# x by ScalarE's queue, first weights in 256 KB pieces, state-space parameters later: a change to the start of a decoder layer's kernel

## The chip, the cores and the metric

The kernel runs on one core of a Trainium2 chip. The core has five engines that run on their own and wait for one another through semaphores: TensorE (PE: matrix products; PEld in the profile is its loading of the stationary operand), VectorE (DVE), ScalarE (ACT), GpSimd (POOL) and SyncE (SP, which here only issues DMAs). DMAs are issued by SP, ACT or POOL from their instruction streams and are carried by 16 DMA engines.

The metric is device time in microseconds (us). Before the change the median of three runs is 1703.63 us.

## The reference

One layer of a decoder on 256 tokens of 2048 numbers. x is multiplied with one wide matrix, three token mixers (S5, GLA, HGRN2) work on the columns, gates merge them, and an MLP follows. Cut to what matters here:

```
h = x @ W_in                        # (256, 2048) @ (2048, 14352), float32
y_a = s5_branch(u_a, lam_re, lam_im, log_dt, b_re, b_im, c_re, c_im, ...)
y_b = gla_branch(q_b, k_b, v_b, ...)        y_c = hgrn2_branch(q_c, f_c, i_c, ...)
merged = sum over branches of sigmoid(gate) * (y @ W_up)
x = layer_norm(alpha * x + merged @ W_out)
x = layer_norm(alpha * x + relu(x @ W1)**2 @ W2)
```

The change touches only the order in which x, the first columns of W_in and the parameters of S5 arrive.

## The kernel before, in words

All products are float32 products made of rounded parts: an operand is split into a high part (ScalarE copies it to a rounded type, `act`, L129) and a low part (VectorE subtracts, `tt`, L107), and three products (high with high, high with low, low with high) give the result. The weights stream through the core once. They come in loads of 1 MB (`emit_dma`, L169 for the first four and L172 for all others), into four raw buffers (NRAW = 4). Each load has two halves of 512 KB, and each half is split (`emit_split`, `emit_lower`) some steps before its products.

The program is one list of steps, written out in order. A step is the products of one half of a load with one of the two token tiles. The first chunk of the list is 512 columns of W_in (the values of GLA): four loads, eight halves, 16 steps of six products each (L1321 to L1323). The chunks that follow it are of the other kind, with 128 columns at a time on the partitions (L1326, L1327).

x has to be turned around before it can be used. `load_x` (L246) loads it in eight pieces of 256 columns (256 KB, 1 KB for each token), and `x_piece` takes one piece through four transposes on TensorE (`transposes`, L134), a copy on ScalarE (L129) and a subtraction on VectorE (L107). The first piece is done ahead of step 0, the seven others in every second step from step 1 to step 13. While the first operands arrive, TensorE multiplies zeros (WARM = 4 products, L228; the profile counts each as two).

At the start SP issues everything that the stream needs: the identity matrix for the transposes (L138), and then by turns one piece of x and half a load of weights, sixteen DMAs in all. GpSimd issues the norm weights of HGRN (`hnw`, L1258), the parameters of S5 (`s5_params`, L279 to L294, thirteen DMAs) and two masks (`load_masks`, L584 and L585).

The work of the token mixers is done by background tasks. They are Python generators; `run_tasks` lets them emit instructions, by priority, as long as an estimate of what VectorE and ScalarE have been given stays below 1240 ns a step. `yield n` makes a task wait for 2 n steps. In the kernel before, `s5_params` issues its DMAs with its first instruction and yields 3; its next part begins with a transpose of the small vectors (L298) on TensorE. `s5_prepare` and `s5_main` wait until `s5_params` is through; the result of S5 is used when its sigmoid unit (`split_z`, `in_s_w_glu_dram`) begins.

Each engine carries out its instructions in the order in which they are emitted, DMA issues among them.

Of the kernel before, what the change touches and what calls it, by code (L numbers as in the profile page):

```python
# [24 lines left out]
WARM = 4           # products of zeros at the start  # L25

# columns of w_in
# [3 lines left out]
# 2*pi in parts of few bits, so that their products with a whole number are exact  # L31
# [7 lines left out]
class Chunk:  # L39
    """A product of weights with activations that are split into rounded parts.  # L40
    rows: 512 columns of the result for each of the two token tiles, tokens on partitions;
    cols: two blocks of 128 columns of the result, these on partitions;
    low: the one block of 16 columns (with 112 that are not used), on partitions."""

    def __init__(self, units, act, evac, kind="rows"):
        self.units = units        # DRAM views [128, k-tiles, columns] of 1 MB
        self.act = act            # k-tile -> its parts
        self.evac = evac          # evac(t, psum)
        self.kind = kind
        self.kpu = units[0].shape[1]  # L50
        self.groups = [[u] for u in range(len(units))]   # units that take tile 0 before tile 1
        self.ps = {}
# [3 lines left out]
def trunk_kernel(ctx: ExitStack, tc, io, out):  # L56
    nc = tc.nc
    V, S, G, T = nc.vector, nc.scalar, nc.gpsimd, nc.tensor

    # ------------------------------------------------------------------ pools  # L60
# [7 lines left out]
    WPG = 8            # pages kept for the weights  # L68
# [27 lines left out]
    # --------------------------------------------- instructions with their cost  # L96
# [34 lines left out]
    def transposes(ps, srcs):  # L131
        """ps [128, 512]: up to four [128, 128] blocks side by side"""
        for i, s in enumerate(srcs):
            T.transpose(ps[:, i * 128:(i + 1) * 128], s, ident)  # L134

    # -------------------------------------------------------------- constants
    ident = cst.tile([128, 128], F32, name="ident")
    nc.sync.dma_start(ident, io["c_eye"])  # L138
    xin = io["x"][0].rearrange("(t p) d -> p t d", p=128)

    w_in = io["w_in"][0]
# [4 lines left out]
    # ---------------------------------------------------------- weight stream  # L146
# [3 lines left out]
    loads = []          # (chunk, ku): 4x128 rows of weights in order of first use  # L150
    order = []          # (chunk, ku, j): halves of them
    steps = []          # (chunk, ku, j, t)
# [4 lines left out]
    def emit_dma():  # L157
        k = dma_n[0]
        if k >= len(loads):
            return  # L160
        c, ku = loads[k]
        r = wp.tile([128, 4, 512], F32, tag="raw", bufs=NRAW, name=f"raw{k}")
        n = c.units[ku].shape[2]
        r4 = r.rearrange("p a b -> p (a b)").rearrange("p (k n) -> p k n", n=n)
        raws[id(c), ku] = r
        dma_n[0] += 1
        if k < NRAW:
            for j in range(2):
                nc.sync.dma_start(r4[:, 2 * j:2 * j + 2], c.units[ku][:, 2 * j:2 * j + 2])  # L169
                yield  # L170
        else:
            nc.sync.dma_start(r4, c.units[ku])  # L172

    late = {}            # the lower parts, a step after the upper ones
# [20 lines left out]
    def emit_lower(n):  # L195
        """those of the halves before n"""
        for k in [k for k in late if k < n]:
            late.pop(k)()

    # ------------------------------------------------------- background tasks  # L200
    tasks = []           # [priority, ready step, generator]
# [13 lines left out]
    def run_tasks(vb, sb):  # L215
        """urgent ones (priority < 0) always; others while the budgets last"""
# [6 lines left out]
    # keep the array busy while the first operands arrive: its clock rises with use  # L223
# [6 lines left out]
    # ------------------------------------------------------ x, its transposes  # L230
    xq = {}          # pairs of k-tiles: [128, 2, (hi, lo), 256 tokens]

    def parts(pages):
        """k-tile -> (hi, lo, both side by side) of pages that hold pairs of k-tiles"""
# [7 lines left out]
    def load_x(ku):  # L242
        xn[ku] = page((128, 2, 512))
        for i in range(2):
            c0 = ku * 512 + i * 256
            nc.sync.dma_start(xn[ku][:, :, i * 256:i * 256 + 256], xin[:, :, c0:c0 + 256])  # L246
            yield

    def split_from_psum(hi, lo, ps, t):
        """psum [128, 4*128] -> columns of token tile t of the pages hi, lo"""  # L250
# [5 lines left out]
    def x_piece(q):  # L256
        """k-tiles 2q, 2q + 1"""
# [10 lines left out]
    # ------------------------------------------------------------ S5 constants  # L268
    S5 = {}

    def s5_params():
        tmp0, tmp1 = page((128, 8, 128)), page((128, 8, 128))
        w = [tmp0[0:32, i, :] for i in range(8)]
# [22 lines left out]
        # per-partition vectors  # L296
# [5 lines left out]
        # lower bound of the forget gates: softmax over the one layer, its running sum less the first  # L302
# [11 lines left out]
        # discretisation, [32 pairs of groups, 128 states]  # L314
# [13 lines left out]
        # the whole number in two parts of few bits  # L328
# [10 lines left out]
        # turns once more into [-1/2, 1/2]  # L339
# [37 lines left out]
        # sine and cosine of theta*t for t = 0..15 and t = 0, 16..240, [128, 2, 32 pairs, 16]  # L377
# [21 lines left out]
        # input matrices [128 = (group of the pair, state), re/im, 32 pairs, 16]  # L399
# [14 lines left out]
        # block-diagonal expansions of four pairs at a time  # L414
# [6 lines left out]
    def s5_prepare():  # L421
        """for each two pairs the stacked operands of B u, which carry float32 products in one
        pass of rounded parts: u as [hi; lo; hi], B^T as [hi; hi; lo], 32 rows each"""
# [44 lines left out]
    uT = {}          # batch-of-four -> page [128 channels, 4, 256]  # L468
    zT = {}
    zq = {}  # L470
    yT = {}          # branch -> {ku: (hi, lo)}

    def s5_tables(hb):
        """sine and cosine of theta*t, [128, 2 pairs, 256], by the sum of angles"""
# [16 lines left out]
    def s5_main():  # L491
# [4 lines left out]
        for hb in range(16):  # L496
# [38 lines left out]
            # s_re = cos zr - sin zi ; -s_im = -cos zi - sin zr  # L535
# [41 lines left out]
    # ------------------------------------------------- gated linear attention  # L577
    masks = {}

    def load_masks():  # L580
        m = cst.tile([128, 5, 128], U8, name="lvl")
# [3 lines left out]
        G.dma_start(dg, io["c_diag"])  # L585
        masks["m"], masks["d"] = m, dg
# [7 lines left out]
    def attention(Q, K, A, need, vsrc, dv, sink):  # L594
        """Q, K, A [128 k, 4 heads, 256 t]; vsrc(t, h) -> [128, dv]; scores by halves of
        blocks of doubling size, each against the decay to the middle of its block. Blocks of
        up to 32 sit side by side on the columns of the array."""
# [92 lines left out]
    def squares(ss, blocks):  # L690
        """sums of squares of blocks [128, n] into the columns of ss"""
# [5 lines left out]
    def rms(ss, n):  # L697
        """1/sqrt(mean of squares + eps)"""
# [5 lines left out]
    def transpose_out(nat, hi, lo, t):  # L704
        """nat [128 tokens, 512] -> columns of tile t in pages hi, lo"""
# [4 lines left out]
    R = {}     # results kept between tasks  # L710

    # GLA -----------------------------------------------------------------
    def ev_copy(key, c, func=AF.Copy, scale=None, dve=False):
        """natural chunk into a page [128, 2, 512]"""
# [6 lines left out]
    def joined(ps, o, scale=None):  # L721
        """o = the two halves of a bank added: products with the high and the low parts"""
# [8 lines left out]
    def ev_page(key, i, func=None, scale=None):  # L731
        """two blocks of columns into blocks 2i, 2i+1 of a page [128, 4, 256 tokens]"""
# [25 lines left out]
    def ev_low(t, ps):  # L758
        """low-rank decay logits, transposed [16, 256]"""
# [6 lines left out]
    def gla_decay(glT):  # L766
        """the decays of GLA, [128, 4 heads, 256]"""
# [51 lines left out]
    # HGRN ----------------------------------------------------------------  # L819
    def ev_f(g, i):  # L820
        """forget gates f of two heads, keys 1 - f"""
# [42 lines left out]
    def branch_out(br):  # L864
        """natural results of a branch to pages with the columns on partitions"""
# [16 lines left out]
    # merge ---------------------------------------------------------------  # L882
# [30 lines left out]
    # ------------------------------------------------------------ layer norms  # L913
# [28 lines left out]
    def normalise(which, t, mv, rs, dve, pool):  # L942
        """rows of tile t; the chunks of dve there, those of pool on ScalarE and GpSimd"""
# [53 lines left out]
    # -------------------------------------------------------------------- MLP  # L997
    hid = {}

    def ev_mlp1_rows(hc):  # L1000
        """512 hidden columns, tokens on partitions"""
# [15 lines left out]
    def ev_mlp1(hc, i):  # L1017
        """blocks 2i, 2i+1 of 512 hidden columns, these on partitions"""
# [39 lines left out]
    # ------------------------------------------------------------ the program  # L1058
    xact = parts(xq)

    def named(pages):
        """k-tile -> parts, of pairs of pages (hi, lo) of four k-tiles"""
# [72 lines left out]
    # sigmoid unit of branch A, columns on partitions  # L1135
# [85 lines left out]
    # pages are released when the last chunk that reads them has been issued  # L1221
# [28 lines left out]
    # start: x and the first weights  # L1250
    for _ in range(NRAW):
        for _ in zip(load_x(dma_n[0]), emit_dma()):
            pass
# [4 lines left out]
    G.dma_start(hnw, io["hgrn_norm_w"].to_broadcast([128, 128]))  # L1258
# [24 lines left out]
    for s, (c, ku, j, t) in enumerate(steps):  # L1283
# [28 lines left out]
        nj = kpu // 2                       # k-tiles in these pages  # L1312
# [36 lines left out]
def _constants():  # L1349
    """depend on shapes alone: identity, which group of a pair a channel row is in, the time  # L1350
    index, and for each block size the pairs (key in first half, query in second half)"""
# [36 lines left out]
```

## Time and profile before

| | before |
|---|---|
| device time, three runs | 1703.1, 1704.76, 1703.63 us; median 1703.63 us |
| span of the profiled execution | 1702.4 us (first to last instruction; the profile gives no other time for it) |
| TensorE busy | 1671.8 us, 98% of the span |
| VectorE, ScalarE, GpSimd busy | 1202.0, 817.3, 190.1 us |
| mean granted TensorE clock | 0.993 of full speed |
| DMA | 318.6 MB, 187 GB/s on average |

A profile is one execution, with times from its first instruction on. A row of a timeline is the start, the duration, the engine (SPq, ACTq, POOLq and POOL's DMA rows are DMA issues), the line of the kernel, the operation, the output and the input by their names in the program, and how many such instructions the row merges. In brackets stands how long the engine had been idle before, and what ended that. The time of a DMA issue is the time the issuing engine spends on it; "to landing" is from the issue to the semaphore that says that all data has arrived. The busy time of TensorE is modelled, since its products are pipelined.

### The profile page before, as it was taken

The page shows a single profiled execution, that of the slowest core. Times are in us where ns is not written, and L with a number is a line of the kernel's source. Part 1 is how long each engine was busy: PE and PEld are TensorE (multiplying, and loading weights), DVE is VectorE, ACT ScalarE, POOL GpSimd, SP SyncE. Part 2 cuts the span into 40 slices and gives each one's busy share as a digit, 9 for nine tenths or more (in the row PEclk, how much of TensorE's full clock was granted, in tenths as well). Part 3 has the DMA queues.
Part 4 walks back from the last instruction along what each step waited for, and adds up shares of the span by engine and source line. Part 5 has one row for each costly group of instructions (what it writes and reads, how often), then busy time and mean ns, then how long its engine had stood idle before and what let it go on. Part 6 is the DMA issues. An engine that isn't in the chain of part 4 may idle for free.

```text
span 1702.4 us, 23554 instructions
## 1 busy us (share of the span) xinstructions
PE 1671.8 (98%) x9390; PEld 1386.8 (81%) x9390; DVE 1202.0 (71%) x1568; ACT 817.3 (48%) x1141; POOL 190.1 (11%) x133
## 2 busy tenths in 40 slices
PE   8999999999999999999999999999999999999996
PEld 6887788887877878878888878888888888888885
DVE  5978889698999999975675756555555555555556
ACT  4463554464535444434644436454455545454540
POOL 2132211021322322100000200000000000000002
PEclk9999999999999999999999999999999999999998
DMA  9555455554556555656585546656655555656651
GB/s 287 188 168 186 154 177 183 159 178 158 179 165 206 187 182 192 204 190 210 168 283 210 179 135 202 194 187 198 198 179 187 188 188 198 198 178 190 226 198 49
DMA packets 218301, 318.61 MB, mean 187 GB/s; under 512 B 8644, under 2 KB 117536, under 8 KB 218192
## 3 DMA queue, kind: packets, MB, share of 16 engines
q1 hardware_dynamic: 213920, 309.43, 55.2%
q10 hardware_dynamic: 3568, 6.46, 1.2%
q0 software_dynamic: 704, 1.24, 0.5%
q8 instruction: 73, 1.20, 0.3%
q14 instruction: 36, 0.29, 0.1%
HBM read 308.70 MB, written 2.10 MB: 183 GB/s over the span
## 4 chain that ended last, share of the span: by engine, by line
PE 90%; DVE 6%; DMA 2%; issue 1%; ACT 1%; SPq 0%; DVEq 0%; ACTq 0%
PE acc L1326 20%; PE acc L1321 19%; PE acc L1323 18%; PE acc L1322 18%; PE acc L1327 10%; DVE pg L107 3%; DMA raw<-in_w_in_dram 1%; DVE hf L107 1%; PE m L552 1%; PE m L134 1%; DVE pg L118 1%; PE m L623 1%; DVE hf L532 1%; ACT pg L129 0%; PE pb L508 0%
## 5 line engine op out<-in xcount | busy, mean ns | idle before, releaser
L107 DVE TENSOR_TENSOR pg<-raw,pg 128x1024 fp32r<-128x1024 f32 (+1 forms) x571 | 708.6, 1258 | 78.5 <-ACT pg L129 37.5
L129 ACT ACTIVATE pg<-raw 128x1024 fp32r<-128x1024 f32 (+1 forms) x571 | 582.5, 1051 | 318.4 <-PE acc L1323 147.2
L1321 PE MATMUL acc<-pg,pg 128*128 128x512 f32 x1504 | 596.8, 397 | 7.4 <-ACT pg L129 4.7
L1323 PE MATMUL acc<-pg,pg 128*128 128x512 f32 x1504 | 589.0, 392 | 2.4 <-DVE pg L107 2.3
L1322 PE MATMUL acc<-pg,pg 128*128 128x512 f32 x1504 | 589.1, 392 | 2.3 <-DVE pg L107 2.2
L1326 PE MATMUL acc<-pg,pg 128*128 128x512 f32 x1552 | 549.3, 399 | 0.0
L1327 PE MATMUL acc<-pg,pg 128*128 128x256 f32 x1552 | 435.6, 281 | 0.0
L1326 PEld LDWEIGHTS acc<-pg,pg 128*128 128x128 f32 x1552 | 291.7, 188 | 71.7 <-issue 0.7
L1321 PEld LDWEIGHTS acc<-pg,pg 128*128 128x128 f32 x1504 | 283.3, 188 | 71.7 <-ACT pg L129 5.9
L1323 PEld LDWEIGHTS acc<-pg,pg 128*128 128x128 f32 x1504 | 283.5, 189 | 63.6 <-DVE pg L107 3.4
L1322 PEld LDWEIGHTS acc<-pg,pg 128*128 128x128 f32 x1504 | 283.6, 189 | 60.9 <-DVE pg L107 5.4
L1327 PEld LDWEIGHTS acc<-pg,pg 128*128 128x128 f32 x1552 | 293.6, 189 | 0.6
L129 ACT ACTIVATE hf<-acc 128x256 f32<-128x256 f32 (+2 forms) x103 | 39.8, 386 | 206.5 <-PE acc L1327 195.7
L107 DVE TENSOR_TENSOR hf<-acc,hf 128x256 f32<-128x256 f32 (+1 forms) x69 | 29.1, 421 | 139.6 <-ACT hf L129 139.6
L951 POOL TENSOR_TENSOR pg<-pg,hf 128x512 f32<-128x512 f32 x7 | 11.4, 1623 | 973.1 <-ACT pg L129 973.1
L107 DVE TENSOR_TENSOR hf<-hf,hf 128x512 f32<-128x512 f32 (+1 forms) x144 | 116.5, 827 | 3.5 <-ACT hf L129 1.6
L107 DVE TENSOR_TENSOR pg<-pg,acc 128x512 f32<-128x512 f32 x56 | 38.3, 684 | 90.2 <-PE acc L1323 90.2
L129 ACT ACTIVATE hf<-hf 128x256 f32<-128x256 f32 (+1 forms) x152 | 68.3, 456 | 23.2 <-DMA hf<-pg 20.4
L129 ACT ACTIVATE pg<-acc 128x512 f32<-128x512 f32 x40 | 23.8, 595 | 115.8 <-PE acc L1323 115.8
L107 DVE TENSOR_TENSOR pg<-pg,pg 128x512 f32<-128x512 f32 (+3 forms) x75 | 51.4, 715 | 26.0 <-PE m L623 13.6
L129 ACT ACTIVATE pg<-m 128x512 fp32r<-128x512 f32 (+3 forms) x51 | 24.6, 502 | 73.5 <-PE m L134 54.4
L107 DVE TENSOR_TENSOR hf<-pb,hf 128x256 f32<-128x256 f32 x128 | 46.4, 414 | 18.7 <-issue 11.6
(129 smaller groups left out, 739.8 us busy)
## 6 DMA issues: line engine op xcount, KB each, us to landing
raw<-in_w_in_dram SPq DMA_DIRECT2D x109, 1024.0 KB, 5.1
raw<-in_w_mlp_in_dram SPq DMA_DIRECT2D x64, 1024.0 KB, 5.8
raw<-in_w_mlp_out_dram SPq DMA_DIRECT2D x64, 1024.0 KB, 5.1
raw<-in_w_up_dram SPq DMA_DIRECT2D x24, 1024.0 KB, 5.1
raw<-in_w_out_dram SPq DMA_DIRECT2D x16, 1024.0 KB, 6.4
raw<-in_w_in_dram SPq DMA_DIRECT2D x8, 512.0 KB, 11.2
raw<-in_s_w_glu_dram SPq DMA_DIRECT2D x4, 1024.0 KB, 6.0
hf<-pg SPq DMA_DIRECT2D x96, 32.0 KB, 3.3
```

What stands on the lines that cost most here:

```text
L107: V.tensor_tensor(o, a, b, op=op)
L118: V.scalar_tensor_tensor(o, a, s, b, op0=op0, op1=op1)
L129: S.activation(o, a, f, **kw)
L134: T.transpose(ps[:, i * 128:(i + 1) * 128], s, ident)
L532: V.tensor_tensor_scan(z[:, i, :], S5["mag"][:, j:j + 1].to_broadcast([128, 256]), z[:, i, :], 0.0, ALU.mult, ALU.add)
L552: T.matmul(yps[r, 0:256], lhsT=W[:, 2 + ri, r], rhs=m[:, i, :], start=ri == 0, stop=ri == 1)
L623: T.matmul(ps[32 * c:32 * c + 32, i * 16:(i + 1) * 16], lhsT=Kf[:, r], rhs=q4[:, :, 1, :], start=True, stop=True)
L1321: T.matmul(ps, lhsT=a[0][:, sl], rhs=wh[:, i, :], start=f, stop=False)
L1322: T.matmul(ps, lhsT=a[0][:, sl], rhs=wl[:, i, :], start=False, stop=False)
L1323: T.matmul(ps, lhsT=a[1][:, sl], rhs=wh[:, i, :], start=False, stop=l)
L1326: T.matmul(ps, lhsT=wh[:, i, n], rhs=a[2], start=f, stop=False)
L1327: T.matmul(ps[:, 0:256], lhsT=wl[:, i, n], rhs=a[0], start=False, stop=l)
```

## The change

The identity matrix and all of x are issued by ScalarE instead of SP. For each of the first four loads, the two pieces of x come first, then the weights: the first load in four pieces of 256 KB, the three others in halves as before. There is one more product of zeros. `s5_params` and `load_masks` begin with a wait of ten steps; the first DMA of `s5_params` writes a buffer of which VectorE sets one column to zero first, so that GpSimd's DMAs start behind that instruction of VectorE. The DMA of `hnw` goes behind those of the masks. Comment lines are left out here, and nothing else differs.

```diff
-WARM = 4
+WARM = 5
...
     ident = cst.tile([128, 128], F32, name="ident")
-    nc.sync.dma_start(ident, io["c_eye"])
+    S.dma_start(ident, io["c_eye"])
...
         if k < NRAW:
-            for j in range(2):
-                nc.sync.dma_start(r4[:, 2 * j:2 * j + 2], c.units[ku][:, 2 * j:2 * j + 2])
+            n = 1 if k == 0 else 2
+            for j in range(0, 4, n):
+                nc.sync.dma_start(r4[:, j:j + n], c.units[ku][:, j:j + n])
                 yield
...
             c0 = ku * 512 + i * 256
-            nc.sync.dma_start(xn[ku][:, :, i * 256:i * 256 + 256], xin[:, :, c0:c0 + 256])
-            yield
+            S.dma_start(xn[ku][:, :, i * 256:i * 256 + 256], xin[:, :, c0:c0 + 256])
...
     def s5_params():
+        yield 5
         tmp0, tmp1 = page((128, 8, 128)), page((128, 8, 128))
+
+        V.memset(tmp1[0:32, 0, 0:1], 0.0)
...
     def load_masks():
+        yield 5
...
         G.dma_start(dg, io["c_diag"])
+        G.dma_start(hnw, io["hgrn_norm_w"].to_broadcast([128, 128]))
...
-    for _ in range(NRAW):
-        for _ in zip(load_x(dma_n[0]), emit_dma()):
-            pass
+    for k in range(NRAW):
+        load_x(k)
+        list(emit_dma())
...
-    G.dma_start(hnw, io["hgrn_norm_w"].to_broadcast([128, 128]))
     x_piece(0)
     emit_split()
```

## Rows read from the trace of the kernel before

**Rows 1.** The page: busy time of each engine, share of the span, instructions
```profile
PE 1671.8 (98%) x9390; PEld 1386.8 (81%) x9390; DVE 1202.0 (71%) x1568; ACT 817.3 (48%) x1141; POOL 190.1 (11%) x133
```
**Rows 2.** Busy time by stretch: length, engines, PEclk, DMA share, GB/s
```profile
6.00:8.00 2.00, 0.00 (x0) 0.00 (x0) 0.69 (x1) 0.36 (x1) 0.58 (x1) 1.00 0.99 355
...
10.00:12.00 2.00, 2.00 (x5) 1.47 (x6) 0.49 (x2) 1.06 (x1) 2.00 (x2) 0.50 1.08 362
```
**Rows 3.** Timeline of the start: zeros, x's first piece, first weights, first products
```profile
1.19 3.78 PE L228 MATMUL m<-wz 128*128 128x256 f32 x8 [1.19 <-DVE epsl L688]
...
4.76 0.96 PE L134 MATMUL m<-ident,pg 128*128 128x128 f32 x4
...
5.76 0.60 ACT L129 ACTIVATE pg<-m 128x512 fp32r<-128x512 f32 x1 [3.74 <-PE m L134]
...
8.35 1.15 ACT L129 ACTIVATE pg<-raw 128x512 fp32r<-128x512 f32 x2 [1.99 <-DMA raw<-in_w_in_dram]
...
9.03 0.79 PE L1321 MATMUL acc<-pg,pg 128*128 128x512 f32 x1 [3.31 <-ACT pg L129]
...
12.54 0.48 PE L1321 MATMUL acc<-pg,pg 128*128 128x512 f32 x1
```
**Rows 4.** The chain that ended last: a set of transposes, the first chunk's last product
```profile
32.03 0.44 PE m L134 x4
...
39.56 0.23 PE acc L1323
```
**Rows 5.** Timeline of SP's queue
```profile
2.16 0.47 SPq L246 DMA_DIRECT2D pg<-in_x_dram  x1
...
9.18 0.37 SPq L246 DMA_DIRECT2D pg<-in_x_dram  x1
...
13.59 3.97 SPq L246 DMA_DIRECT2D pg<-in_x_dram  x1
```
**Rows 6.** That DMA of 2.16 to landing; queues in 15.8 to 22.3 (packets, MB)
```profile
pg<-in_x_dram SPq DMA_DIRECT2D x1, 256.0 KB, 7.0
...
q0 software_dynamic: 225, 0.75, 69.2%
q1 hardware_dynamic: 220, 0.30, 37.2%
```
**Rows 7.** Timeline of GpSimd's queue: S5's first DMA, the first mask
```profile
1.95 0.54 POOL L279 DMA_DIRECT2D pg<-in_s_lam_re_dram  x1
...
14.76 0.56 POOL L584 DMA_DIRECT2D hf<-in_c_level_dram  x1
```
**Rows 8.** Timeline of SP and ACT from 871 on; SP's first load there to landing
```profile
871.37 3.29 SPq L172 DMA_DIRECT2D raw<-in_w_out_dram  x2
...
880.90 0.33 ACTq L923 DMA_DIRECT2D hf<-in_ln_g_dram  x1
...
881.83 1.06 ACT L129 ACTIVATE pg<-raw 128x1024 fp32r<-128x1024 f32 x1 [8.65 <-DMA hf<-in_ln_b_dram]
...
raw<-in_w_out_dram SPq DMA_DIRECT2D x1, 1024.0 KB, 9.5
```
**Rows 9.** ACT's first loads of x at 847.04; the DMA's stretch behind them
```profile
847.04 0.91 ACTq L995 DMA_DIRECT2D pg<-in_x_dram  x2
...
848.00:850.00 2.00, 2.00 (x10) 1.68 (x9) 2.00 (x3) 2.00 (x3) 0.00 (x0) 1.00 0.84 197
```
**Rows 10.** S5's small vectors, to landing
```profile
vec<-in_hgrn_lb_logits_dram POOLq DMA_DIRECT2D x1, 4.0 KB, 5.7
```
**Rows 11.** The end of S5 on ACT; the loads of its sigmoid unit
```profile
759.84 1.06 ACT L129 ACTIVATE pg<-pg 128x1024 f32<-128x1024 f32 x1 [9.16 <-DVE pg L118]
...
L172 SPq DMA_DIRECT2D raw<-in_s_w_glu_dram x4: 367/368/368, 779.4 to 794.7; - x4
```
**Rows 12.** Busy time by stretch, 40 to 100 us (PE, PEld, DVE, ACT, POOL)
```profile
40.00:60.00 20.00, 20.00 (x117) 17.19 (x116) 18.18 (x47) 10.88 (x16) 0.00 (x0) 1.00 0.68 218
...
80.00:100.00 20.00, 18.01 (x101) 15.13 (x100) 19.95 (x22) 7.04 (x10) 14.70 (x10) 1.00 0.40 133
```

## The prediction

> **What bounds the kernel now.** I read the page first: TensorE is busy 98% of the span [rows 1]. A change at the start can only move the moment from which the products run back to back; a microsecond won there is one won at the end, as long as nothing later stops TensorE. The timeline of the start and the chain give that moment. The first product starts at 9.03, after ScalarE has copied the first weights, for which it had waited until 8.35 [rows 3]; the first chunk's last product ends at 39.56 + 0.23 = 39.79 [rows 4]. The chunk thus takes 30.76 us. Its work is 96 products of 0.23 and seven further sets of transposes of 0.44 [rows 4], 22.1 + 3.1 = 25.2 us, so 5.6 us are lost. Of these 1.7 are the clock: TensorE was idle from 5.72 (4.76 + 0.96) to 9.03, its granted clock stood at 0.50 (1.2 GHz) in 10 to 12 [rows 2], and the first six products with one set of transposes, 1.8 us of work, took the 3.5 us from 9.03 to 12.54 [rows 3]. The other 3.9 are waits for operands.
>
> Why they are late is in the stretches and the queues. The DMA moves 355 to 362 GB/s where hardly anything but SP's queue runs [rows 2], but in 15.8 to 22.3, beside GpSimd's large DMAs, 225 packets of GpSimd's queue moved 0.75 MB and 220 of SP's only 0.30 [rows 6].
>
> One more thing matters here: an issue can wait. SP's issue at 9.18 came when the piece of x of 2.16 landed (2.16 + 7.0), eight DMAs earlier [rows 5, 6]. ScalarE and SP share that count: ScalarE's issue at 880.90 came when SP's load of 871.37 landed (871.37 + 9.5), and ScalarE's next copy stood idle 8.65 us behind its own issues [rows 8].
>
> **The change part by part.** *x by ScalarE.* ScalarE gets nine issues ahead of its first copy. Counted over both queues in the program's order, the sequence is the identity, two pieces of x, four of weights, two of x, two halves, two of x, two halves, two of x, two halves. By eights, x's last piece waits for x's fourth to land, x's fifth and sixth for the first two pieces of weights. So ScalarE's first copy, that of x's first piece, comes only when x's fourth piece has landed and one more issue is through. SP's side is not hurt: it loses nine issues and has nothing else to do.
>
> When does x's fourth piece land? The first issue stays near 0.74, where the first engine's issue is now. Bytes flow about 1.0 us after an issue, and for two us at 197 GB/s [rows 9], then at the full rate; at 362 [rows 2] that equals full rate from 0.74 + 1.0 + 0.9 = 2.65. ScalarE's queue must move 64 + 4 x 256 = 1088 KB. If SP's queue moves as many bytes beside it, 2176 KB take 6.0 us: landing at 8.65. If the two take turns by packets, as GpSimd's and SP's did by count (225 and 220 [rows 6]), x's rows of 1 KB go one for one with the weights' rows of 2 KB; then the first load's 1024 KB and about 860 of the second pass as well, 2970 KB, 8.2 us: 10.85. Then one issue (0.47 [rows 5]), x's copy (0.60) and, from the copy of the weights to the product, 0.68 (8.35 to 9.03 [rows 3]): 1.75 in all. **First product: 10.4 or 12.6.** I take 11.5, the middle, because the rows of equal counts speak of two queues of different kinds, and no row shows two like queues with rows of different lengths. That is 2.5 us later than now.
>
> *The waits after it.* At 362 GB/s a half with its piece of x (768 KB) takes 2.1 us, its products and transposes 2 x 1.38 + 0.44 = 3.2. Without GpSimd's DMAs beside them all 6.06 MB are in by 2.65 + 16.7 = 19.4, and the last half is needed at 11.5 + 7 x 3.2 = 33.9. So the 3.9 us of waits go. The loss to the clock stays 1.7, since TensorE is idle even longer; the fifth product of zeros (3.78 / 4 = 0.95, ending at 5.9 [rows 3]) ends long before the first product and costs nothing. The first chunk ends at 11.5 + 25.2 + 1.7 = 38.4 (37.3 to 39.5) instead of 39.79: **-1.4 us (-2.5 to -0.3).** Weights in pieces of 256 KB are two more issues on SP and worth nothing here, since ScalarE is held for longer than the first piece needs.
>
> *S5's parameters ten steps later.* GpSimd's sixteen DMAs move behind an instruction of VectorE near step 12, at about 11.5 + 1.7 + 12 x 1.6 = 32.4. Nothing on SP waits for them; the loads beside them have three raw buffers of 1 MB as a lead, which covers a stretch of slower DMA. Their readers: the small vectors are the first seven issues, 7 x 0.54 = 3.8 us [rows 7], and land 5.7 later [rows 10], at 41.9; TensorE transposes them at step 19, 38.4 + 3 x 1.4 = 42.6. That is 0.7 us of cover, and each us beyond it is a wait. The masks are issued 12.8 after the first (1.95 to 14.76 [rows 7]), at 45.2; even with 9.5 to land, as SP's load took in [rows 8], they are there at 54.7, and VectorE copies them at step 33 or later, 38.4 + 17 x 1.4 = 62. S5 as a whole ends up to ten steps of 1.6 later, 760.9 + 16 = 776.9; the first weights that meet its result are issued at 779.4 [rows 11], so that is covered too.
>
> What is not covered is VectorE. S5's first small instructions move out of the first chunk into a stretch where it is busy 18.18 of 20 us; and in 80 to 100, at 19.95 of 20, TensorE already loses 2.0 [rows 12]. Bounds: +2.0 if such a wait comes once more, -2.0 if this one goes. I take +0.5, near none, because TensorE lost nothing in 40 to 60 at 18.18.
>
> **Sum:** -1.4 + 0.5 = -0.9 us. The profiled execution's 1702.4 become 1701.5. The median of the runs is 1.2 above its span, so I forecast **1702.7**, with a range of its own of 1700 to 1705.5. 0.2% of this kernel, about what a measurement can tell from no change, is 3.4 us, so this is no change.
>
> **The rivals.** *ScalarE is not held.* If its issues only cost their own time, nine of 0.47 from 0.74 end at 5.0. The zeros end at 5.9, transposes, copy and split take 0.96 + 0.60 + 0.68: first product at 8.2. The idle time before it is then short; after 2.3 us of idle (5.72 to 8) the clock was still 1.00 [rows 2], so the 1.7 are saved too: first chunk done at 33.4, -6.4 + 0.5 = -5.9, **1697.7**. For it: only one stretch shows ScalarE held by its own issues. Against it: there the landing of SP's load fits to 0.1 us. The Trainium skill, "DMA: Bandwidth & Descriptors", section "Issuing engines are not separate DMA queues", says that starting DMAs on several engines only saves the time that a sequencer spends on issuing, usually small beside the transfer. By that rule ScalarE's issues would cost their own time and the sum would be this rival's; the 8.65 us of [rows 8] do not agree with it. Chance 0.22.
>
> *ScalarE is held still longer*, and the kernel is slower. Place: its last issue of x. On SP this same piece's issue, at 13.59, took 3.97 us instead of 0.47 [rows 5]. With turns by packets the first product is then at 12.6 + 3.5 = 16.1 and the chunk's end at 43.0: +3.2 + 0.5 = +3.7, **1707.3**. It decides from a first product at 15.8 on. For it: as many DMAs are in flight then as at 13.59. Against it: GpSimd was just then issuing its large DMAs, and they are gone. Chance 0.13.
>
> **How the numbers follow.** Forecast 0.65, the rivals 0.22 and 0.13. Faster by over 0.2% (below 1700.2): most of the first rival and a tail of the forecast (turns by bytes, and the wait at 80 to 100 gone), 0.20 + 0.05 = 0.25. Slower (above 1707.0): most of the second and a small tail, 0.11 + 0.03 = 0.14. Within: 0.61. The range goes from the first rival's time to the second's, 1697.5 to 1707.5; about 2 in 10 lie outside, mostly beyond the rivals' own sums.
>
> **What would show it.** Right: ScalarE's first copy idle until about 9 to 11.5, behind its last issue of x, which starts when x's fourth piece lands; the first product at 10.4 to 12.6; granted clock 0.50 for some us behind it; no wait of TensorE from there to the chunk's end at 37.3 to 39.5; DMA near 360 GB/s until about 19; the small vectors landing before TensorE transposes them. Wrong: a first product before 9 (first rival) or after 15.8 (second); waits of TensorE for VectorE in 60 to 160 that grow by more than 2.0; or a wait for the small vectors.

## The result, and the profile after

The changed kernel takes 1719.68 us, median of four runs (1717.85 to 1721.42), against 1703.45 for the kernel before beside it: a ratio of 1.0095 with an interval of 1.0083 to 1.0107. That is 16 us slower, and 12 above the range. The profiled execution has a span of 1716.1 (1717.85 us in all), 13.7 more than before.

The page of the changed kernel (busy time of each engine with its share and instructions, which answers to [rows 1], and the shares of the chain that ended last):

```profile
PE 1676.3 (98%) x9392; PEld 1388.6 (81%) x9392; DVE 1202.1 (70%) x1569; ACT 819.5 (48%) x1142; POOL 192.5 (11%) x133
...
PE 81%; DVE 13%; issue 2%; DMA 2%; ACT 1%; SPq 0%; ACTq 0%; DVEq 0%
```

In the kernel before, that last line was:

```profile
PE 90%; DVE 6%; DMA 2%; issue 1%; ACT 1%; SPq 0%; DVEq 0%; ACTq 0%
```

TensorE is busy only 4.5 us longer than in [rows 1], but VectorE's share of the chain has gone from 6 to 13%: the end now hangs more often on a piece of VectorE. Where, the stretches tell (length, then busy time of PE, PEld, DVE, ACT and POOL with instructions, granted clock, DMA share, GB/s). The changed kernel:

```profile
0.00:45.00 45.00, 38.46 (x168) 30.76 (x169) 20.50 (x27) 20.01 (x28) 11.07 (x19) 0.92 0.82 264
...
88.00:764.00 676.00, 661.62 (x4383) 536.32 (x4383) 589.90 (x813) 324.01 (x441) 157.54 (x99) 0.99 0.54 174
```

and the kernel before in the same two:

```profile
0.00:45.00 45.00, 38.52 (x168) 29.68 (x169) 25.11 (x49) 21.29 (x30) 11.77 (x20) 0.96 0.99 285
...
88.00:764.00 676.00, 669.79 (x4450) 544.96 (x4449) 596.75 (x825) 322.73 (x438) 146.74 (x94) 1.00 0.54 180
```

The start came out even. The loss lies in 88 to 764, where S5 runs: TensorE stands 676.00 - 661.62 = 14.4 us there, before 676.00 - 669.79 = 6.2. Counting the accumulators' products in order, the 385th starts 0.6 us later than before (at 91), the 3,073rd 15.2 later (758.4 against 743.2); near 1000 us 2.2 come back, and the rest stays to the end. In between the products do not fall behind in one place: by 6.0 us at the 601st (134 us in the kernel before), by only 2.7 at the 651st (147 us, where the kernel before stands too), by 7.1 at 372 us, 11.2 at 579 and 14.8 at 653.

**The start.** The timeline of the changed kernel answers to [rows 3], and the chain's last line to the last line of [rows 4]:

```profile
1.17 8.37 ACTq L247 DMA_DIRECT2D pg<-in_x_dram  x8
...
1.19 4.63 PE L229 MATMUL m<-wz 128*128 128x256 f32 x10 [1.19 <-DVE epsl L693]
...
9.58 1.28 ACT L129 ACT_TABLE_LOAD   x1 [9.58 <-DMA pg<-in_x_dram]
10.87 0.60 ACT L129 ACTIVATE pg<-m 128x512 fp32r<-128x512 f32 x1
...
12.04 0.80 PE L1325 MATMUL acc<-pg,pg 128*128 128x512 f32 x1 [5.33 <-ACT pg L129]
...
39.55 0.23 PE acc L1327
```

ScalarE does nothing but issue until 9.55, then loads its table of functions, and only then copies. The first product comes 3.0 us later than before; the first chunk ends at 39.55 + 0.23 = 39.78, as before (39.79), because no wait is left in it.

**What TensorE waited for** in 88 to 764 (engine, line, releaser: us in total, times, longest). The changed kernel, then the kernel before:

```profile
PE m L628 <- DVE pg L107: 4.7, 4, 1.8
PE acc L1326 <- DVE pg L107: 2.7, 3, 1.9
PE acc L1325 <- DVE pg L107: 2.5, 3, 1.3
PE acc L1331 <- DVE pg L107: 2.3, 2, 1.2
PE acc L1330 <- DVE pg L107: 2.0, 3, 1.1
```

```profile
PE acc L1321 <- DVE pg L118: 2.2, 1, 2.2
PE m L134 <- DVE s5eb L433: 1.1, 1, 1.1
PE m L134 <- DVE s5ec L112: 0.9, 1, 0.9
```

All 14.2 us of the first list are waits for VectorE: for splits of weights and the emptying of accumulators (acc), and for the operands of attention's scores (m L628). The first of them, in the stretches of the changed kernel:

```profile
96.00:100.00 4.00, 2.85 (x16) 2.26 (x16) 4.00 (x4) 0.00 (x0) 3.92 (x4) 1.00 0.00 0
100.00:104.00 4.00, 4.00 (x15) 2.89 (x15) 4.00 (x5) 2.39 (x5) 3.92 (x3) 0.75 0.01 4
104.00:108.00 4.00, 4.00 (x20) 3.42 (x20) 3.97 (x6) 1.40 (x3) 3.92 (x4) 0.83 0.67 215
108.00:112.00 4.00, 1.88 (x10) 1.14 (x8) 4.00 (x4) 3.95 (x6) 2.65 (x2) 1.00 0.14 47
112.00:116.00 4.00, 3.80 (x13) 3.26 (x14) 3.46 (x5) 3.97 (x4) 0.00 (x0) 0.57 0.77 236
```

VectorE is full from 96 to 112, TensorE stands 1.15 + 2.12 us, and the granted clock falls to 0.75, 0.83 and 0.57. Over 88 to 764 the low clock costs 4 x (0.25 + 0.17 + 0.43) in these rows and 4 x 0.43 once more at 648 to 652, 5.1 us; before it cost 1.7 (at 144 to 152). Standing and clock thus account for (14.4 + 5.1) - (6.2 + 1.7) = 11.6 of the 14.6 us by which the products fall behind there. The other 3 are in neither count. Part of them can be that a wait also spreads the pipelined products around it: over the wait at 98.91 two products start 1.55 us apart instead of 0.23, which is 0.17 more than the 1.15 counted as idle. At that size the 15 waits of the first list against 8 of all kinds before would make some 1.2 us, an estimate; the rest stays open.

What VectorE, TensorE and GpSimd did there (timeline of the changed kernel by engine):

```profile
89.81 1.22 DVE L107 TENSOR_TENSOR pg<-raw,pg 128x1024 fp32r<-128x1024 f32 x1
...
91.54 2.15 DVE L107 TENSOR_TENSOR hf<-pg,p 128x512 f32<-128x512 f32 x2
93.61 3.24 DVE L107 TENSOR_TENSOR pg<-pg,p 128x512 f32<-128x512 f32 x2
96.77 2.08 DVE L107 TENSOR_TENSOR pg<-raw,pg 128x1024 fp32r<-128x1024 f32 x1
...
99.11 2.88 DVE L107 TENSOR_TENSOR pg<-pg,hf 128x512 f32<-128x512 f32 x2
...
102.19 1.80 DVE L107 TENSOR_TENSOR pg<-raw,pg 128x1024 fp32r<-128x1024 f32 x1
103.91 1.14 DVE L436 COPY s5eb<-pg 64x64 f32<-64x64 f32 x2
...
108.37 3.45 DVE L107 TENSOR_TENSOR pg<-raw,pg 128x1024 fp32r<-128x1024 f32 x2
111.74 0.41 DVE L107 TENSOR_TENSOR pg<-acc,hf 128x256 f32<-128x256 f32 x1
...
98.91 0.39 PE L1331 MATMUL acc<-pg,pg 128*128 128x256 f32 x1 [1.15 <-DVE pg L107]
...
112.20 0.80 PE L1330 MATMUL acc<-pg,pg 128*128 128x512 f32 x1 [1.14 <-DVE pg L107]
...
91.71 1.43 POOL L485 TENSOR_TENSOR hf<-pg 128x512 f32<-128x512 f32 x1 [46.00 <-DVE pg L114]
...
108.44 2.29 POOL L490 TENSOR_TENSOR hf<-hf,hf 128x512 f32<-128x512 f32 x1
```

Between the split of 89.81 and that of 96.77 stand large pieces of S5's parameters (91.54 and 93.61), between that and the split of 102.19 the last two (99.11); behind that of 102.19 the first pieces of S5's loop (s5eb, s5ec). GpSimd makes S5's tables beside them from 91.71 to 110.7. TensorE uses a split up in some 2.8 us, and these come 5 to 7 us apart. VectorE does not have more to do in the changed kernel: it is busy 1202.1 us in all, before 1202.0. What has changed is when its pieces come.

### The profile page after: what moved, and what is told of

Its sections match the earlier page's. It is cut to its first block, busy times and chain, and to the rows that moved or that the text cites. A ratio compares the mean times of both kernels' runs of the same rounds, so it can differ in the third digit from the quotient of the medians.

```text
span 1716.1 us, 23572 instructions
## 1 busy us (share of the span) xinstructions
PE 1676.3 (98%) x9392; PEld 1388.6 (81%) x9392; DVE 1202.1 (70%) x1569; ACT 819.5 (48%) x1142; POOL 192.5 (11%) x133
## 4 chain that ended last, share of the span: by engine, by line
PE 81%; DVE 13%; issue 2%; DMA 2%; ACT 1%; SPq 0%; ACTq 0%; DVEq 0%
PE acc L1330 18%; PE acc L1325 17%; PE acc L1326 17%; PE acc L1327 17%; PE acc L1331 9%; DVE pg L107 7%; DVE hf L107 3%; DVE hf L535 1%; DVE pg L118 1%; PE m L134 1%; ACT pg L129 1%; DMA raw<-in_w_in_dram 1%; PE m L555 1%; PE m L628 1%; DMA pg<-in_x_dram 0%
## 5 line engine op out<-in xcount | busy, mean ns | idle before, releaser
L956 POOL TENSOR_TENSOR pg<-pg,hf 128x512 f32<-128x512 f32 x7 | 11.4, 1627 | 972.0 <-ACT pg L129 972.0
L107 DVE TENSOR_TENSOR hf<-hf,hf 128x512 f32<-128x512 f32 (+1 forms) x144 | 109.8, 780 | 4.9 <-ACT hf L129 2.9
L485 POOL TENSOR_TENSOR hf<-pg 128x512 f32<-128x512 f32 x16 | 23.7, 1479 | 324.3 <-DVE hf L107 94.9
```

The source lines that it names most:

```text
L107: V.tensor_tensor(o, a, b, op=op)
L485: G.tensor_tensor(co, coarse(cs), fine(cs), op=ALU.mult)
```

## The experiments

**Which part of the change.** The first four runs take it apart. The first undoes the two lines that write S5's parameters and the masks ten steps later, and keeps the start:

```diff
     def s5_params():
-        yield 5
...
     def load_masks():
-        yield 5
```

> The changed kernel without the two waits of ten steps; x by ScalarE, the pieces of 256 KB, the fifth product of zeros, VectorE's store ahead of S5's DMAs and the late norm weights stay. Theory A (the loss is S5's place in the written order: moved ten steps later, its pieces meet VectorE between 90 and 720 us where TensorE then waits): the order is that of the kernel before again, and only the start is left, which stood at +0.35 us at the 128th product: 1703.5 to 1705.5, PE waits on DVE between 100 and 800 as before, some 4 us. Theory B (the loss comes from the start: ScalarE held and late parameters leave a lag that later stages carry): stays slow, 1714 or more.

Measured: 1704.21 against 1704.24, ratio 1.0000 (0.9991 to 1.0010). The first product starts at 11.94. The start of the change alone is worth nothing in either direction, and the whole loss hangs on the two lines. The second run has only these two lines, on the kernel before:

```diff
     def s5_params():
+        yield 5
...
     def load_masks():
+        yield 5
```

> The kernel before with nothing but the two waits of ten steps in s5_params and load_masks. Theory A: 1716 to 1720, with the same growth of TensorE's lag after 90 us as the changed kernel. Theory B: 1702 to 1705, since x, the weights and ScalarE are as before.

Measured: 1717.26, ratio 1.0077 (1.0062 to 1.0092). The first product starts at 8.67, and the first chunk ends 1.5 us earlier than before; that is less than what is lost afterwards. GpSimd's DMAs are not behind the chunk here: without VectorE's store ahead of them they are issued as early as before (the first large one at 9.02, before at 9.64), so this run moves S5's computing and leaves its loads. The loss is the same all the same: from the 385th to the 3,073rd product it falls 14.4 us further behind the kernel before, and the changed kernel 14.6. In the medians the two runs make 0 and 13 us, the whole change 16; the intervals of 13 and 16 overlap, and the 1.5 us of the first chunk are a part of the difference. The third and the fourth run have one of the two lines each:

```diff
     def s5_params():
+        yield 5
```

> The kernel before with the wait of ten steps in s5_params alone; the masks stay early. If S5's place is the cause: 1714 to 1720. If the masks' place is: 1702 to 1705.

```diff
     def load_masks():
+        yield 5
```

> The kernel before with the wait of ten steps in load_masks alone; S5 stays early. If S5's place is the cause: 1702 to 1705. If the masks' place is (their five small copies then stand elsewhere in VectorE's order): 1714 to 1720.

Measured: with S5's parameters late 1717.17, ratio 1.0072 (1.0057 to 1.0087); with the masks late 1702.22, ratio 0.9991 (0.9982 to 1.0001). It is S5's parameters alone. The list of waits of this third kernel is nearly that of the changed one:

```profile
PE m L624 <- DVE pg L107: 4.7, 4, 1.8
PE acc L1328 <- DVE pg L107: 3.7, 2, 2.5
...
```

**Does the loss grow with the lateness?** Four steps and twenty, and the loop alone ten later (its two tasks wait ten steps behind the parameters, which stay in their place):

```diff
     def s5_params():
+        yield 2
```

> The kernel before with S5's parameters four steps later instead of ten (yield 2). If lateness itself is the cause, in proportion (13 us for ten steps): about 5 us, 1708 to 1711. If it is how S5's pieces happen to fall against the other work of VectorE: any time between 1702 and 1718, not on the line between none and ten.

```diff
     def s5_params():
+        yield 10
```

> The kernel before with S5's parameters twenty steps later (yield 10). Lateness in proportion: +26 us, about 1730, or more than ten steps cost at the least. The way the pieces fall: no order with the ten steps, any time between 1702 and 1722.

```diff
         yield from wait_for("par")
+        yield 5
         EB, EC = S5["EB"], S5["EC"]
...
         yield from wait_for("par")
+        yield 5
         yield from room("hf", 4)
```

> The kernel before with a wait of ten steps in s5_prepare and s5_main behind S5's parameters: these and their large table products stay where they are, the sixteen rounds of S5's loop come later. If the loss is made by the loop's rounds (TensorE's lag grew by some 10 us between 200 and 750): 1712 to 1718. If it is made where the parameters' end meets the start of GLA, at 90 to 125: 1703 to 1707.

Measured: four steps 1717.23, ratio 1.0077 (1.0062 to 1.0092); twenty 1708.48, ratio 1.0027 (1.0016 to 1.0038); the loop alone 1703.94, ratio 0.9997 (0.9987 to 1.0007). The loss does not grow with the lateness: four steps cost as much as ten, and twenty cost a third. The third is what is left of two things. With twenty steps S5's DMAs are issued only behind the first loads, instead of from 1.95 on [rows 7]:

```profile
26.18 0.53 POOL L280 DMA_DIRECT2D pg<-in_s_lam_re_dram  x1 [23.12 <-DMA raw<-in_w_in_dram]
```

The first product starts at 9.08, as before, but TensorE is then busy for all of 10 to 40 (before: 28.01 of 30 us), and the chunk ends 3.4 us earlier than in the kernel before. Counted from the 129th product on, behind the chunk, the profiled executions with four, ten and twenty steps lose 11.9, 14.5 and 8.0 us: less far apart, but still not in order. Nor is a late loop dear in itself. With it TensorE stands as little from 88 to 764 as before, 6.1 us:

```profile
88.00:764.00 676.00, 669.87 (x4444) 544.19 (x4443) 588.27 (x823) 321.87 (x438) 142.31 (x94) 1.00 0.55 180
```

**Two steps either way, and parameters and loop both late.** If the loss comes of the parameters' last pieces and the loop's first meeting at 96 to 112, moving the loop away from the late parameters should cure it.

```diff
     def s5_params():
+        yield 5
...
         yield from wait_for("par")
+        yield 5
         EB, EC = S5["EB"], S5["EC"]
...
         yield from wait_for("par")
+        yield 5
         yield from room("hf", 4)
```

> The kernel before with the parameters ten steps later (as in the run with these alone, 1717.2) and the loop's two tasks ten steps later again, behind the parameters. In that run TensorE stood 2.4 + 1.2 us at 96 to 112 and its clock was low up to 116, some 6.5 us; with the loop alone ten steps later nothing was lost there. Theory 1 (parameters and the loop's first pieces together crowd VectorE): the loss at 96 to 116 falls to 2 us or less, and the time to 1706 to 1712. Theory 2 (the parameters alone crowd it, against GLA's decays): the loss at 96 to 116 stays 5 to 7 us, and the time stays at 1714 to 1719.

```diff
     def s5_params():
+        yield 1
```

> The kernel before with the parameters two steps later. If the loss grows step by step with the place: 1705 to 1709, between the kernel before and four steps (1717.2). If the field is rough (what counts is which pieces meet, not how late): anything from 1700 to 1718, and at four or ten steps the loss says nothing of it.

```diff
     def s5_params():
...
-        yield 3
+        yield 2
         ps = psm()
```

> The kernel before with the parameters' second piece two steps earlier; the loop's first rounds are written at nearly the same steps as before. If earlier is always safer: 1702 to 1704.5. If the field is rough: 1704.5 to 1715.

Measured: both late 1720.56, ratio 1.0098 (1.0084 to 1.0112); two steps later 1703.18, ratio 0.9995 (0.9986 to 1.0004); two steps earlier 1709.01, ratio 1.0027 (1.0017 to 1.0037; its profiled span, 1702.4, shows less of this than its other runs). Three stretches of the kernel with both late, and of the one two steps later:

```profile
96.00:116.00 20.00, 18.84 (x103) 15.63 (x102) 17.34 (x18) 13.71 (x17) 15.24 (x9) 1.00 0.34 107
276.00:290.00 14.00, 11.24 (x164) 8.81 (x163) 12.21 (x13) 5.45 (x6) 4.04 (x3) 0.88 0.50 155
384.00:400.00 16.00, 11.56 (x163) 9.01 (x163) 14.71 (x15) 4.50 (x5) 6.46 (x4) 0.79 0.43 135
```

```profile
96.00:116.00 20.00, 20.00 (x114) 17.04 (x112) 10.18 (x11) 15.76 (x20) 9.92 (x5) 1.00 0.57 177
276.00:290.00 14.00, 13.55 (x181) 10.79 (x180) 13.91 (x16) 7.87 (x9) 4.51 (x3) 1.00 0.60 197
384.00:400.00 16.00, 16.00 (x252) 12.65 (x251) 14.86 (x21) 6.24 (x8) 0.00 (x0) 1.00 0.63 206
```

With both late the crowding at 96 to 116 did shrink as the first theory had it (1.16 us of standing at full clock). But the loop's later rounds then met other work: 2.76 us stand at 276 to 290 and 4.44 at 384 to 400, with the clock down, and the time is the worst of all. Both are one kind of wait, that of attention's scores for VectorE (sum, times and longest over 88 to 764):

```profile
PE m L626 <- DVE pg L107: 7.2, 2, 4.4
```

So the time I expected from that theory was missed by 8 us or more, and the reading that the loss is made only at 90 to 125 fell with it. What holds in all these runs is that the parameters' places two and four steps later differ by 14 us, and all places tried by up to 17, not in order of lateness, and that in the stretches shown the difference is TensorE standing for VectorE. Which pieces must not meet was not found; only that single meeting at 96 to 116 was taken apart.

**More splits in hand.** If the splits are late only for a moment, one more half of the weights split ahead (2.8 us of TensorE's work) should bridge it:

```diff
-        ... LA + 4 * (s > 660))
+        ... LA + 2 * (s < 300 or 400 < s < 600) + 4 * (s > 660))
```

> The changed kernel whole, but with one more half of the weights split ahead (look-ahead 8 steps in place of 6) in steps 14 to 299 and 401 to 599; up to step 300 (some 510 us) every other task is written at the same step as in the changed kernel. From 88 to 764 us that kernel's TensorE stood 14.4 us and its low clock cost 5.1; before: 6.2 and 1.7. Theory (the late S5 pieces delay splits on VectorE for a short while, and four halves in hand do not bridge it): the waits for splits before 510 us go, with the clock they cost: about 13 of the 19.5 us, so 1705 to 1709. Rival (VectorE is full there, so that a split written earlier only makes something else late; the waits move to the scores of attention, L628): 1715 to 1720.

> The kernel before with the same one more half ahead. Its own 7.9 us of standing and low clock from 88 to 764 are mostly waits for S5's own operands (s5eb, s5ec, 2.0) and one for L118 (2.2), which splits in hand do not shorten. Theory: 1700 to 1704. Rival (more in hand makes other pieces late): 1704 to 1708.

> The start with x on both queues (1699.8, the fastest so far) with the same one more half ahead. Theory: the parts are independent, so its time lies as far below that start alone as the kernel before with one more half lies below the kernel before: 1696 to 1700. Rival (the deeper look-ahead costs as much as it gives): 1700 to 1704.

Measured: the changed kernel 1716.42, ratio to before 1.0071 (1.0059 to 1.0084); the kernel before 1708.39, ratio 1.0026 (1.0016 to 1.0035); the start with x on both queues 1705.63, ratio 1.0007 (0.9998 to 1.0016). My theory fell: some 3 us of 16 come back in the changed kernel, within the rival's range, and the other two get 4 and 6 us slower, 0.4 and 1.6 beyond their rivals' ranges. The waits did not move to attention's scores, as the first rival had it (L628: 3.7 us instead of 4.7). The timeline of the first (VectorE, then TensorE) shows the wait taking another form:

```profile
106.43 2.00 DVE L436 COPY s5eb<-pg 64x64 f32<-64x64 f32 x2
108.44 1.37 DVE L112 TENSOR_SCALAR s5ec<-pg,gmask 128x128 f32<-128x128 f32 x1
109.73 2.35 DVE L107 TENSOR_TENSOR pg<-raw,pg 128x1024 fp32r<-128x1024 f32 x2
112.00 0.41 DVE L107 TENSOR_TENSOR pg<-acc,hf 128x256 f32<-128x256 f32 x1
...
112.47 0.80 PE L1330 MATMUL acc<-pg,pg 128*128 128x512 f32 x1 [3.86 <-DVE pg L107]
```

The splits are in time now, and TensorE stands 3.86 us in one piece for an accumulator that VectorE empties at 112.00, behind S5's operands and behind two splits which, with more in hand, should not be needed yet. Here it is VectorE's order that is late, whatever TensorE has in store.

**A start that keeps ScalarE free.** ScalarE issues only the identity and x's first two pieces; SP issues the rest of x among the weights, and the two lines are undone. The last run adds the masks' line, which alone cost nothing.

```diff
-            S.dma_start(xn[ku][:, :, i * 256:i * 256 + 256], ...)
+            (S if ku == 0 else nc.sync).dma_start(xn[ku][:, :, i * 256:i * 256 + 256], ...)
...
     def s5_params():
-        yield 5
...
     def load_masks():
-        yield 5
```

> The changed kernel without its two waits of ten steps, and ScalarE issues only the identity and the first two pieces of x; the six others go by SP ahead of their weights, as in the list. If ScalarE's hold is what made the first product late (12.0): ScalarE is free at about 2.5, its table load ends at 4, the first product comes at 7.5 to 9 and the first chunk ends 3 to 5 us earlier, 1699 to 1701.5 in all. If data were late anyway: first product at 11 to 12, 1703 to 1705.

```diff
     def load_masks():
+        yield 5
```

> The start with ScalarE issuing the identity and two pieces of x (1699.8), and the masks ten steps later (alone: 1702.2 against 1704). If the parts add up: 1697 to 1700. If the masks' place matters only through the S5 pieces beside them: 1699 to 1706.

Measured: 1699.81, ratio 0.9976 (0.9967 to 0.9986), and with the masks late 1697.80, ratio 0.9965 (0.9953 to 0.9978): both faster than both kernels. The timeline of the last one's start:

```profile
1.16 0.99 ACTq L247 DMA_DIRECT2D pg<-in_x_dram  x2
...
2.19 1.28 ACT L129 ACT_TABLE_LOAD   x1 [2.19 <-issue]
...
7.64 0.49 PE L1324 MATMUL acc<-pg,pg 128*128 128x512 f32 x1 [1.21 <-ACT pg L129]
```

ScalarE is free at 2.2, its table loads while it would wait anyway, and the first product starts at 7.64, 4.4 us before the changed kernel's. The first chunk's last product starts at 35.04 instead of 39.39 in the changed kernel. Against the kernel before, the first product is only 1.4 us earlier; the other 3 us of the chunk are its waits, which are gone. S5's large DMAs, behind VectorE's store, go from 20.96 on here instead of from 9.64, which fits the run with twenty steps; no run has this start with those DMAs early.

## Why the prediction was wrong

The forecast was no change at 1702.7; its own sum had -1.4 us for the start and +0.5 for S5. The start gave 0.0, S5 and what follows it gave some 13.

- **The hold of ScalarE: right.** Its first copy came behind its own last issue of x, the first product at 12.04, within the 10.4 to 12.6 given. x's last issue, at 9.17, came when x's third piece landed (2.18 + 7.0), not the fourth, as I had counted (4.23 + 7.2 = 11.4). Had it waited for the fourth, the first product would have come 2.3 us later, at 14.3 and outside what I gave: that the number fits is in part luck.
- **A term that was missing there:** ScalarE's table of functions. In the kernel before it loads in ScalarE's idle time; here it stands behind the issues and takes 1.28 us at 9.58, on the path. Without it the first product is at 10.8, near the lower end.
- **The waits in the first chunk: right**, all 3.9 us went. The run with twenty steps bears out the reason, GpSimd's DMAs: its products start as early as before and yet hardly wait, now that these go behind the first loads. The chunk ends 3.4 us earlier there, and 1.2 with ten steps, where only S5's computing has left it (one profiled execution each). My sum for the loads mixed two units (6208 KB of 1024 bytes are 6.36 MB, not 6.06, so 20.2 and not 19.4; the last half landed at 21.0), and nothing hung on it.
- **The clock: mis-sized.** It stayed at 0.50 from 12.04 to about 16.6 (0.84 as the mean of 16 to 18), so that it cost 2.3 us instead of the 1.7 taken over from before (granted clock over the first 45 us 0.92, before 0.96). With the 0.5 by which the first product came later than my 11.5, that takes 1.1 of the 1.4 us back. The 1.7 was also one execution's: in the kernels with the two lines alone and with two steps the first product came at 8.67 and 8.59, but 0.50 lasted to about 14.9 and 14.5 (0.77 and 0.88 as the means of 14 to 16), which is 3.1 and 2.9.
- **S5's parameters: the covers held, VectorE did not.** The small vectors landed well ahead (the last at 37.34 + 3.9 = 41.2, TensorE took them at 43.93 without a wait). S5 ended 17.9 us later (its last function at 777.78), and the weights that meet its result were issued at 794.6 instead of 779.4, so 16.8 of the 19.6 us between the two were left and S5's end held nothing up.
- **The step that failed** is this: "What is not covered is VectorE. ... Bounds: +2.0 if such a wait comes once more, -2.0 if this one goes. I take +0.5, near none, because TensorE lost nothing in 40 to 60 at 18.18." The stretch that I looked at stayed clean; TensorE was busy for all of 40 to 60 in the changed kernel too. But the ten steps moved all that follows from the parameters, their large pieces and sixteen rounds of the loop, over some 670 us, and I bounded it by one wait of [rows 12]. That row, TensorE losing 2.0 where VectorE is busy 19.95 of 20, was the warning: VectorE can be without slack where S5 meets the rest, and [rows 12] covers 60 us of it. With the right stretch (88 to 764, VectorE busy 597 of 676) the bound belonged to the sum over all its meetings there, not to one. In the runs with the parameters alone moved it lay between nothing (two steps later: -0.9, within the noise) and +13 us (four or ten).
- **The rivals.** A held ScalarE came as forecast, so the first rival fell. The Trainium skill ("DMA: Bandwidth & Descriptors", "Issuing engines are not separate DMA queues") says that starting DMAs on several engines only saves the sequencer's time for issuing; read as in the prediction, ScalarE's issues would have cost only their own time. The trace does not agree: nine issues of 0.37 to 0.66, 4.0 us in all, took until 9.55. The second rival, a first product beyond 15.8, did not come, and the kernel is slower for another reason than its. The sign that I named, waits for VectorE in 60 to 160 growing by more than 2.0, did not come either: their sum is 4.2 us in both kernels, in other places. The products are some 3 us late by 160, and most of the loss lies behind the stretch that I would have watched.

## What to carry to other kernels

Where one program order, written ahead, feeds several engines, a few steps of delay for a background task are no small edit: it shifts every later piece of that task against everything else on the busiest in-order queue, and the cost is a sum over the whole task, to be tried at several places rather than argued. Undo such a line by itself before judging the edit that it came with: here it hid a start that was neutral, and that became 4 us faster than the kernel before once ScalarE issued only what is needed first. Nor does such a line always move the same things: with VectorE's store it moved S5's loads and its computing, without the store, at ten steps, the computing alone. An engine whose computing is on the path at the start issues only the transfers that it needs itself, and its table of functions loads before a wait and not behind one.

## What was not expected of the hardware

- The load of ScalarE's table comes in its queue's order: at 0.74 in the kernel before, at 2.19 behind three issues, at 9.58 behind nine. It took 1.28 each time.
- After short stands the granted clock did not always fall. Before, TensorE stood 1.05 and 0.93 us at 92 to 96, and 96 to 100 ran at 1.00; in the changed kernel it stood 1.19 and 1.14 at 108 to 112, and 112 to 116 ran at 0.57. What decides between the two was not tried.
- VectorE's split of a half, 1.22 us at 89.81, took 2.08 at 96.77 and 1.80 at 102.19, beside GpSimd's tables. That agrees with the Trainium skill, "GPSIMD Engine Reference", "1. Specifications": GpSimd shares its interfaces to the on-chip buffer (SBUF) with VectorE, with contention where a VectorE instruction has two inputs there. Over the whole trace of the changed kernel 527 such splits with no product of GpSimd beside them took 1.15 to 1.26 us, and the 30 with one beside them for nearly all of their time 1.21 to 2.32, 1.97 in the median. No run took the tables away, so it is the rows alone that say it. VectorE's busy time in all is the same in both kernels, so it does not explain the loss by itself.
